# The opening of both feed-forward blocks of an encoder layer, put into one written order with six pairs begun early

## The chip, the cores and the metric

The kernel runs on one core of one Trainium2 chip. The time is the device time of one execution in microseconds (us). TensorE (PE) multiplies matrices, with a weight load (PEld) ahead of each matmul; VectorE (DVE) and ScalarE (ACT) work on elements; SyncE (SP) issues most of the transfers (DMA). Each of these engines takes its instructions in the order of its own queue.

## The reference

One layer of a bidirectional encoder, in float32, for two groups of tokens (512 and 256, together 768) of width 1024:

```python
def swiglu(x, w_up, w_down):
    gate, up = jnp.split(x @ w_up, 2, axis=-1)
    return (jax.nn.silu(gate) * up) @ w_down

x = layer_norm(ALPHA * x + 0.5 * swiglu(x, ffn1_up, ffn1_down), ln1_g, ln1_b)
u = x @ w_in
...                       # RWKV-7 branch h_a, retention branch h_b, gates
mix = (jax.nn.sigmoid(gate_a) * h_a + jax.nn.sigmoid(gate_b) * h_b) @ w_out
x = layer_norm(ALPHA * x + mix, ln2_g, ln2_b)
x = layer_norm(ALPHA * x + 0.5 * swiglu(x, ffn2_up, ffn2_down), ln3_g, ln3_b)
```

The hidden width of a feed-forward block is 2816, which is 22 column blocks of 128. The change concerns the two `swiglu` blocks alone, called block 1 and block 2 below.

## The kernel before

**Precision.** Every operand of a large product is kept as two parts, a rounded one (`ph`, `xh`, `eh`) and the rest (`pl`, `xl`, `el`). `split` (L196) makes them: ACT casts the source to the rounded part (L197), then DVE subtracts it from the source (L198). One product is then three sets of matmuls: rounded weights by both parts of the tokens, and the rest of the weights by the rounded tokens.

**Pairs and products.** `ffn` (L310) works on 22 pairs, one for each block of 128 hidden columns: the gate and the up weights of that block. The inner width (8 slabs of 128) and the tokens (768) are each cut in two, so the tokens are four quarters: B11 and B21 are the first 384 tokens of slabs 0-3 and 4-7, B12 and B22 the last 384 tokens. A pair's 2x2 by 2x2 product is done with seven products instead of eight, from sums of quarters and sums of weight halves. A product takes 4 slabs, so it has 12 matmuls over 384 tokens. They are numbered as in the code: 1 and 2 use plain weights and B11, B21; 5, 7, 6, 3 use weight sums (made by `combine`, L357, on DVE into `sa` tiles) with the token forms T1, T3, T2 and with B22; 4 uses plain weights with the form T4.

**Token forms.** `forms` (L290) makes T1 to T4 once a block: 16 DVE subtractions (4 slabs by 4 forms), and a split of each result, which is 16 casts on ACT and 16 subtractions on DVE, all of 128x384. In block 1 twelve splits of token quarters come on top (L1262); in block 2 the layer norm ahead of it has made them.

**Order.** A planner, which knows the durations only by a model, orders the instructions of each engine by readiness, with older ones first. Where `manual_schedule` is used (L524) PE, ACT and DVE keep the written order among the instructions of that region; how these fall among others of the same engine stays with the planner. Before the change, the loads, the token forms and the products 1 and 2 of the first four pairs (`head` L362, `second` L371, LEAD = 4) stand ahead of the region, so the planner orders them. The region (`body`, L483) runs a list of items, one product each. In its step t it does this: `post` of item t-1 (copies, SiLU and additions from PSUM), loads, weight sums that are needed some items later, the weight split (`prep`) of item t+2, the late part of item t-1, and the matmuls of item t. An early pair has five items left (5, 7, 6, 3, 4), another pair has seven. The weight pieces have four buffers each, raw weights ten. After each chunk of pairs (6, 6, 5, 5) come the items of the down product (`down_items`).

**Around block 2.** Layer norm 2 (L264, in two halves of 384 tokens) ends just as block 2 begins. The weights of block 2 are loaded once the buffers of the stage before are free, and PSUM is handed from one pool to the next.

Of the kernel before, what the change touches and what calls it, by code (L numbers as in the profile page):

```python
# [18 lines left out]
P = 128  # L19
# [36 lines left out]
LEAD = 4  # L56
# [13 lines left out]
class Builder:  # L70
# [219 lines left out]
    def forms(self, z, xs, ext, tmp):  # L290
        nc = self.nc
        m = KT // 2
        sub = lambda o, a, b: nc.vector.tensor_tensor(out=o, in0=a, in1=b, op=ALU.subtract)
        B = [[t[:, c:c + TH] for t in (z[k], z[k + m]) for c in (0, TH)] for k in range(m)]
        ta = [tmp.tile([P, T], F32, tag="hh", name=self.nm("f")) for k in range(m)]
        for k, (b11, b12, b21, b22) in enumerate(B):
            sub(ta[k][:, :TH], b12, b11)
            self.split(ta[k][:, :TH], *(t[:, TH:] for t in xs[k]))
        tb = [tmp.tile([P, T], F32, tag="hl", name=self.nm("f")) for k in range(m)]
        for k, (b11, b12, b21, b22) in enumerate(B):  # L300
            sub(tb[k][:, :TH], b22, b12)
            self.split(tb[k][:, :TH], *(t[:, :TH] for t in ext[k]))
        for k, (b11, b12, b21, b22) in enumerate(B):
            sub(ta[k][:, TH:], b22, ta[k][:, :TH])
            self.split(ta[k][:, TH:], *(t[:, 2 * TH:] for t in ext[k]))
        for k, (b11, b12, b21, b22) in enumerate(B):
            sub(tb[k][:, TH:], b21, ta[k][:, TH:])
            self.split(tb[k][:, TH:], *(t[:, TH:2 * TH] for t in ext[k]))

    def ffn(self, ctx, z, xs, idx, up, down, after, lead, first, then=None):  # L310
# [6 lines left out]
        hs, raws, open_ = {}, {}, {}  # L317
# [25 lines left out]
        def load(j, part):  # L343
            if (j, part) not in raws:
                raws[j, part] = raw(up[j, :, part])
            return raws[j, part]
# [7 lines left out]
        def product(ps, w, x, start):  # L354
            self.mmt(ps, self.terms(pieces(w), X[x]), ((0, TH),), start, True, not start)

        def combine(a, b, op):  # L357
            t = fw.tile([P, m * P], F32, tag="sa", name=self.nm("sa"), bufs=4)
            nc.vector.tensor_tensor(out=t, in0=a, in1=b, op=op)  # L359
            return t  # L360

        def head(j):  # L362
            g = load(j, 0)
            s, uu = (hp.tile([P, T], F32, tag=t, name=self.nm("u")) for t in ("hh", "hl"))
            ps = self.bank()[:, :TH]
            product(ps, g[0], "11", True)
            nc.scalar.copy(uu[:, :TH], ps)  # L367
            open_[j] = s, uu, ps
            return g

        def second(j, g):  # L371
            s, uu, ps = open_[j]
            product(ps, g[1], "21", False)
            nc.scalar.activation(s[:, :TH], ps, AF.Silu)

        def pair_items(j):
            early = j in open_
            st = {}

            def sums(names):  # L380
                def run():
                    (g0, g1), (u0, u1) = load(j, 0), load(j, 1)
                    for n in names:
                        if n == 1:
                            st[1] = combine(u0, u1, ALU.add)
                        elif n == 3:
                            st[3] = combine(g0, u0, ALU.subtract)
                        elif n == 2:
                            st[2] = combine(st[1], g0, ALU.subtract)
                        else:  # L390
                            st[4] = combine(g1, st[2], ALU.subtract)
                return run

            if early:
                st["s"], st["u"] = open_[j][:2]
# [11 lines left out]
            src = {1: lambda: load(j, 0)[0], 2: lambda: load(j, 0)[1], 4: lambda: load(j, 1)[1],  # L407
# [26 lines left out]
            def after_late(n):  # L434
                if n == 4:
                    nc.vector.tensor_tensor(out=hs[j][1], in0=st["s"], in1=hs[j][0].bitcast(F32), op=ALU.subtract)
                    for k in ((j, 0), (j, 1)):
                        raws.pop(k)

            items = []  # L440
            of = {5: 1, 7: 3, 6: 2, 3: 4}
            for n in (5, 7, 6, 3, 4) if early else (1, 5, 7, 6, 2, 3, 4):
# [4 lines left out]
                need = (sums((of[n],)), 3 if early else 6 + (n in (6, 3))) if n in of else None  # L447
                items.append((src[n], mm, *(lambda n=n, f=f: f(n) for f in (post, late, after_late)), need))
            return items, lambda: (load(j, 0), load(j, 1))

        def down_items(ci):
            ch = chunks[ci]
            items, fetch = [], []
            for n in range(KT):
                got = {}
                for i, c in enumerate(range(0, len(ch), m)):
# [22 lines left out]
                    items.append((get, mm, post, none, none, None))  # L479
                    fetch.append(get)  # L480
            return items, fetch

        def body():  # L483
            items, fetch, extra, mixed = [], {}, {}, []
            for ci, ch in enumerate(chunks):
                for q, j in enumerate(ch):
                    its, get = pair_items(j)
# [89 lines left out]
        if then:  # L577
            then()
# [778 lines left out]
```

## Time and profile before

| | |
|---|---|
| median of 3 runs | 1981.83 us (1980.63 to 1992.86) |
| profiled execution: its own time | 1982.73 us |
| its span, first to last instruction | 1981.0 us |
| PE busy | 1886.8 us (95%) |
| DVE busy | 1259.4 us (64%) |
| ACT busy | 807.0 us (41%) |
| mean granted clock of PE | 0.979 |
| block 1: first matmul, start of the 43rd product | 5.80, 107.07 us |
| block 2: first matmul, start of the 43rd product | 1431.88, 1527.43 us |

Busy times are sums over the span. An instruction's duration includes the tail of its pipeline, so an engine that issues without a pause has starts that are closer together than its durations are long. In rows of the timeline, the columns are the start, the duration, the engine, the line, the operation, the tiles written and read, the shapes and the count; a bracket at the end tells how long the engine stood idle before it, and what released it. Rows of stretches (windows) give, after the length, the busy time and the number of instructions of PE, PEld, DVE, ACT and POOL, then the granted clock, the share of the DMA engines and GB/s.

### The profile page before, as it was taken

How to read it: one execution, taken by the hardware profiler on the slowest of the kernel's cores; microseconds unless marked ns; L12 is line 12 of the kernel's file. 1: busy time of each engine (PE TensorE's matmuls, PEld its weight loads, DVE VectorE, ACT ScalarE, POOL GpSimd, SP SyncE). 2: the span in 40 equal slices, each digit the busy share in tenths (PEclk: the TensorE clock that was granted, in tenths of full speed). 3: DMA queues.
4: the chain of work that ended last, by engine and by line, in shares of the span. 5: the costliest groups of instructions: out<-in, count | busy, mean ns of one | idle time of the engine just before them, and what ended most of it. 6: DMA issues, size and time to landing. Idle time of an engine off the chain costs nothing.

```text
span 1981.0 us, 33145 instructions
## 1 busy us (share of the span) xinstructions
PE 1886.8 (95%) x13098; PEld 1685.0 (85%) x13098; DVE 1259.4 (64%) x2208; ACT 807.0 (41%) x1521; POOL 190.3 (10%) x290
## 2 busy tenths in 40 slices
PE   7999999999989999999899989999899999999997
PEld 7999999998778778887688867789789899899985
DVE  8855746656745686768445555386797477375655
ACT  6422423323454353545255555332554234132325
POOL 0000000000000365345610000000000000000000
PEclk9999999999989999999999989999999999999998
DMA  5222222121332433333555442654222221222221
GB/s 197 81 69 75 64 75 71 49 85 45 123 103 69 156 115 127 116 128 121 155 164 139 123 121 74 210 163 138 80 77 73 81 69 56 79 63 69 67 70 66
DMA packets 140444, 198.40 MB, mean 100 GB/s; under 512 B 55552, under 2 KB 73600, under 8 KB 140288
## 3 DMA queue, kind: packets, MB, share of 16 engines
q1 hardware_dynamic: 122752, 174.25, 27.8%
q0 software_dynamic: 3424, 14.94, 2.2%
q10 hardware_dynamic: 14112, 7.08, 1.3%
q8 instruction: 104, 1.70, 0.4%
q14 instruction: 52, 0.43, 0.1%
HBM read 154.54 MB, written 41.68 MB: 99 GB/s over the span
## 4 chain that ended last, share of the span: by engine, by line
PE 82%; DVE 9%; ACT 4%; DMA 3%; issue 2%; SPq 0%; ACTq 0%; POOL 0%; DVEq 0%; POOLq 0%
PE mm L208 39%; PE pc L208 30%; PE pc L253 2%; PE mm L630 2%; PE pc L107 2%; PE pc L1046 1%; DMA t<-gd 1%; PE w L982 1%; PE pc L1094 1%; PE pc L687 1%; DVE z L281 1%; PE w L993 1%; DVE u L410 1%; PE w L987 1%; PE pc L1055 1%
## 5 line engine op out<-in xcount | busy, mean ns | idle before, releaser
L208 PE MATMUL pc<-xh,ph 128*128 128x384 f32 x704 | 241.9, 344 | 20.8 <-ACT u L367 6.7
L208 PE MATMUL pc<-xl,ph 128*128 128x384 f32 x704 | 237.8, 338 | 0.1
L197 ACT CAST ph<-wr 128x512 fp32r<-128x512 f32 (+1 forms) x232 | 131.1, 568 | 220.2 <-PE mm L208 140.3
L208 PE MATMUL mm<-xh,wh 128*128 128x512 f32 (+1 forms) x640 | 177.2, 356 | 15.0 <-DVE t L707 5.1
L410 DVE TENSOR_TENSOR u<-u,pc 128x384 f32<-128x384 f32 x220 | 121.6, 553 | 89.1 <-PE pc L208 85.4
L208 PE MATMUL pc<-el,ph 128*128 128x384 f32 x528 | 176.4, 334 | 0.0
L208 PE MATMUL pc<-eh,ph 128*128 128x384 f32 x528 | 176.4, 334 | 0.0
L208 PE MATMUL mm<-xl,wh 128*128 128x512 f32 (+1 forms) x640 | 169.9, 346 | 0.0
L208 PEld LDWEIGHTS pc<-xh,ph 128*128 128x128 f32 x704 | 133.7, 190 | 30.4 <-ACT u L367 8.0
L198 DVE TENSOR_TENSOR pl<-wr,ph 128x512 fp32r<-128x512 f32 (+1 forms) x232 | 141.6, 623 | 20.6 <-ACT ph L197 20.6
L208 PE MATMUL pc<-xh,pl 128*128 128x384 f32 x704 | 151.0, 336 | 0.0
L198 DVE TENSOR_TENSOR pl<-sa,ph 128x512 fp32r<-128x512 f32 x176 | 121.2, 689 | 45.6 <-ACT ph L197 45.4
L208 PE MATMUL mm<-hl,ph 128*128 128x512 f32 (+1 forms) x544 | 138.9, 336 | 0.0
L208 PE MATMUL mm<-hh,ph 128*128 128x512 f32 (+1 forms) x544 | 138.8, 336 | 0.0
L208 PEld LDWEIGHTS pc<-xl,ph 128*128 128x128 f32 x704 | 133.8, 190 | 0.8 <-DVE xl L198 0.7
L169 DVE TENSOR_TENSOR wl<-wr,wh 128x1024 fp32r<-128x1024 f32 (+1 forms) x68 | 74.8, 1100 | 92.7 <-PE mm L208 47.2
L208 PEld LDWEIGHTS mm<-xh,wh 128*128 128x128 f32 x640 | 101.7, 192 | 36.9 <-issue 14.9
L197 ACT CAST ph<-sa 128x512 fp32r<-128x512 f32 x176 | 105.4, 617 | 52.9 <-DVE sa L359 24.9
L208 PEld LDWEIGHTS pc<-xh,pl 128*128 128x128 f32 x704 | 125.7, 189 | 0.0
L208 PE MATMUL mm<-xh,wl 128*128 128x512 f32 (+1 forms) x640 | 124.2, 343 | 0.0
L168 ACT CAST wh<-wr 128x1024 fp32r<-128x1024 f32 (+1 forms) x68 | 62.7, 922 | 139.0 <-PE mm L208 112.7
L208 PEld LDWEIGHTS mm<-xl,wh 128*128 128x128 f32 x640 | 100.6, 192 | 16.8 <-issue 2.5
(311 smaller groups left out, 3926.3 us busy)
## 6 DMA issues: line engine op xcount, KB each, us to landing
wr<-in_f1u SPq DMA_DIRECT2D x96, 256.0 KB, 3.1
wr<-in_f2u SPq DMA_DIRECT2D x96, 256.0 KB, 3.0
wr<-in_w_in SPq DMA_DIRECT2D x30, 512.0 KB, 3.5
wr<-in_f1d SPq DMA_DIRECT2D x37, 256.0 KB, 2.7
wr<-in_f2d SPq DMA_DIRECT2D x37, 256.0 KB, 2.7
wr<-in_w_in SPq DMA_DIRECT2D x32, 256.0 KB, 3.4
dd<-ar SPq DMA_DIRECT2D x8, 768.0 KB, 3.3
dd<-kb SPq DMA_DIRECT2D x8, 768.0 KB, 4.4
```

What stands on the lines that cost most here:

```text
L107: self.nc.tensor.matmul(ps, w, x[:, a:b], start=True, stop=True)
L168: nc.scalar.copy(hi, raw)
L169: nc.vector.tensor_tensor(out=lo, in0=raw, in1=hi.bitcast(F32), op=ALU.subtract)
L197: self.nc.scalar.copy(hi, src)
L198: self.nc.vector.tensor_tensor(out=lo, in0=src, in1=hi.bitcast(F32), op=ALU.subtract)
L208: self.latest = self.nc.tensor.matmul(o, w, x[:, a:b], start=start and i == 0, stop=stop and i == len(terms) - 1, skip_group_check=more).ins
L253: self.summed = nc.tensor.matmul(st["ps"], self.ones, src, start=k == 0, stop=k == KT - 1).ins
L281: nc.vector.scalar_tensor_tensor(out=zk, in0=zk, scalar=-0.5, in1=rs, op0=ALU.mult, op1=ALU.mult)
L410: add = lambda o, a, b: nc.vector.tensor_tensor(out=o, in0=a, in1=b, op=ALU.add)
L630: nc.tensor.matmul(dst, x[:, ts], w[:, :, k % 4], start=(k == 0 and q == 0), stop=(k == KT - 1 and q == 2))
L687: nc.tensor.matmul(op, v[:, a // P + j], x[:, j, :n], start=(j == 0 and q == 0), stop=(j == nj - 1 and q == 2))
L982: nc.tensor.matmul(pb[64 * h:64 * h + 64, C * j:C * j + C], sc[:, c % 4, h, 1], vu[:, c % 4, h], start=True, stop=True)
```

## The change

The opening moves into the region. `forms` no longer issues anything: it returns a list of single steps. A step is either the start of one form (for T1 to T4 the DVE operation and the cast on ACT, for plain quarters the cast alone) or the DVE subtraction that ends it; each subtraction stands behind the start of the next form. A new function, `advance`, issues steps in the region's step t, behind the weight split of item t+2: up to three DVE operations a step from t = 4 in block 1 (`own` is True: it also splits its own quarters) and from t = 6 in block 2, and more where an item's form would otherwise be missing.

LEAD becomes 6. The list begins with twelve items, products 1 and 2 of pairs 0 to 5 in the order OPEN, then takes the early pairs two at a time: 5, 5, 7, 7, 6, 6, 3, 4, 3, 4. Full pairs have the order 1, 5, 7, 6, 2, 3, 4 with nothing of another pair mixed in. T2 is made as T3 + B11 instead of B22 - T1, and T4 as B21 - T2, as before. Sums of early pairs overwrite their `sa` tile; product 6 of an early pair goes to another PSUM bank. Raw weights are loaded by halves, and the gate weights of six early pairs are loaded twice (of four before). In block 1 the weight and token loads have a new order, and the constants are loaded in step 100.

```diff
-LEAD = 4
+LEAD = 6
+OPEN = [(1, 0), (1, 1), (1, 2), (1, 3), (2, 0), (2, 1), (1, 4), (1, 5), (2, 2), (2, 3), (2, 4), (2, 5)]
+FORMS = {True: 4, False: 6}
...
-    def forms(self, z, xs, ext, tmp):
+    def forms(self, z, xs, ext, tmp, own):
...
+        rows = []
+        if own:
+            rows += [("11", None, B[k][0], part(xs, k, 0)) for k in range(m)]
+            rows += [("21", None, B[k][2], part(xs, k + m, 0)) for k in range(m)]
+        ta, tb = half("hh"), half("hl")
+        rows += [("T1", tt(ta[k], B[k][1], B[k][0], ALU.subtract), ta[k], part(xs, k, TH)) for k in range(m)]
+        rows += [("T3", tt(tb[k], B[k][3], B[k][1], ALU.subtract), tb[k], part(ext, k, 0)) for k in range(m)]
+        rows += [("T2", tt(tb[k], tb[k], B[k][0], ALU.add), tb[k], part(ext, k, 2 * TH)) for k in range(m)]
+        if own:
+            rows += [("22", None, B[k][3], part(xs, k + m, TH)) for k in range(m)]
+        rows += [("T4", tt(tb[k], B[k][2], tb[k], ALU.subtract), tb[k], part(ext, k, TH)) for k in range(m)]
+        steps, late = [], None
+
+        def low(src, hi, lo):
+            return lambda: nc.vector.tensor_tensor(out=lo, in0=src, in1=hi.bitcast(F32), op=ALU.subtract)
+
+        for name, make, src, (hi, lo) in rows:
+            def begin(make=make, src=src, hi=hi):
+                if make:
+                    make()
+                nc.scalar.copy(hi, src)
+            if late and name == "21" != late[0]:
+                steps.append(late)
+                late = None
+            steps.append((name, begin, bool(make), False))
+            if late:
+                steps.append(late)
+            late = name, low(src, hi, lo), True, True
+        return steps + [late]
...
-                    st[key] = self.bank()[:, :TH]
+                    st[key] = self.mmps()[:, :TH] if early and n == 6 else self.bank()[:, :TH]
...
-            for n in (5, 7, 6, 3, 4) if early else (1, 5, 7, 6, 2, 3, 4):
+            for n in (1, 5, 7, 6, 2, 3, 4):
...
+            early = [pair_items(j) for j in range(LEAD)]
+            items += [early[j][0][n] for n, j in OPEN]
+            for j in range(0, LEAD, 2):
+                pair = early[j:j + 2]
+                fetch.setdefault(len(items), []).extend(p[1] for p in pair)
+                items += [p[0][n] for n in (5, 7, 6) for p in pair] + [p[0][n] for p in pair for n in (3, 4)]
...
+            steps = self.forms(z, xs, ext, hp, own)
+
+            def advance(t):
+                x = items[t][7] if 0 <= t < len(items) else None
+                names = [n for n, *_ in steps]
+                must = len(names) - names[::-1].index(x) if x in names else 0
+                begin = FORMS[own]
+                n = 0
+                while steps and (must > 0 or n < (3 if t >= begin else 0) or steps[0][0] == "11"
+                                 or steps[0][0] == "21" and t >= 0 and n < 2):
+                    name, f, vector, _ = steps.pop(0)
+                    f()
+                    n += vector
+                    must -= 1
...
                     prep(t + 2)
+                    advance(t)
                     if t > 0:
                         items[t - 1][3]()
...
-        first(load, ext, hp)
-        for j in range(lead):
-            second(j, head(j))
-            raws.pop((j, 0))
+        if start:
+            start(load)
...
             for a in (0, TH):
-                load(a // TH, 0)
-                for k in range(KT):
-                    zk = z[k][:, a:a + TH]
-                    nc.sync.dma_start(zk, I["xT"][:, k, a:a + TH])
-                    if a == 0 or k >= KT // 2:
-                        self.split(zk, *(t[:, a:a + TH] for t in xs[k]))
-            self.forms(z, xs, ext, tmp)
+                for h in range(2):
+                    load(0, 0, h)
+                    for k in range(KT // 2 * h, KT // 2 * (h + 1)):
+                        nc.sync.dma_start(z[k][:, a:a + TH], I["xT"][:, k, a:a + TH])
+                    if a == 0:
+                        for j in range(1, 4 - 2 * h):
+                            load(j, 0, h)
```

More of the change, by code (lines that the diff above doesn't have):

```diff
@@ L303, in forms @@
[L303 to L310, printed above, removed]
+        part = lambda ts, k, c: tuple(t[:, c:c + TH] for t in ts[k])
@@ L311, in ffn @@
+        return steps + [late]
+    def ffn(self, ctx, z, xs, idx, up, down, after, start, own, then=None):
         nc = self.nc
@@ L341, in wide, with load @@
             return tuple(t.rearrange("p (a b) -> p a b", b=P) for t in (h, l))
[L343 to L346, printed above, removed]
+        def load(j, part, h):
+            if (j, part, h) not in raws:
+                raws[j, part, h], = raw(up[j, :, part, h * m:h * m + m])
+            return raws[j, part, h]
         def pieces(src):
@@ L352, in pieces @@
             return tuple(t.rearrange("p (a b) -> p a b", b=P) for t in (h, l))
[L354 to L359, printed above, removed]
-            return t
[L362 to L374, printed above, removed]
+        def combine(a, b, op, out=None):
+            t = fw.tile([P, m * P], F32, tag="sa", name=self.nm("sa"), bufs=4) if out is None else out
+            self.mark = nc.vector.tensor_tensor(out=t, in0=a, in1=b, op=op).ins
+            return t
         def pair_items(j):
-            early = j in open_
+            early = j < LEAD
@@ L378, in pair_items, with sum_of @@
             st = {}
-            def sums(names):
+            def sum_of(n):
                 def run():
[L382 to L391, printed above, removed]
-                return run
@@ L394, in pair_items @@
-            if early:
-                st["s"], st["u"] = open_[j][:2]
+                    g0, g1, u0, u1 = [load(j, p, h) for p in range(2) for h in range(2)]
+                    if n == 1:
+                        st[1] = combine(u0, u1, ALU.add)
+                    elif n == 3:
+                        st[3] = combine(g0, u0, ALU.subtract)
+                    elif n == 2:
+                        st[2] = combine(st[1], g0, ALU.subtract, st[1] if early else None)
+                    else:
+                        st[4] = combine(g1, st[2], ALU.subtract, st[2] if early else None)
@@ L446, in mm @@
                     self.mmt(ps, self.terms(w, X[xof[n]]), ((0, TH),), n not in (2, 3, 4), True, n in (2, 3, 4))
-                need = (sums((of[n],)), 3 if early else 6 + (n in (6, 3))) if n in of else None
-                items.append((src[n], mm, *(lambda n=n, f=f: f(n) for f in (post, late, after_late)), need))
-            return items, lambda: (load(j, 0), load(j, 1))
+                    if early and n < 3:
+                        raws.pop((j, 0, n - 1))
+                need = (sum_of(of[n]), 3 if early else 6 + (n in (6, 3))) if n in of else None
+                get = (lambda n=n: load(j, 0, n - 1)) if early and n < 3 else None
+                items[n] = src[n], mm, *(lambda n=n, f=f: f(n) for f in (post, late, after_late)), need, get, xof[n]
+            return items, lambda: [load(j, p, h) for p in range(2) for h in range(2)]
         def down_items(ci):
             ch = chunks[ci]
-            items, fetch = [], []
+            items = []
             for n in range(KT):
@@ L530, in body @@
                     ahead(t)
+                    if then and t == 100:
+                        with self.tc.issue_after(self.mark):
+                            then()
                     for f in extra.get(t, ()):
@@ L1246, in build @@
                      lambda seg, mean, lp: self.layer_norm(lp, z, 3, None, seg, mean, O["y"]),
-                     LEAD, lambda load, ext, tmp: self.forms(z, self.xs, ext, tmp))
+                     None, False)
     def first(self, ctx):
```

57 lines of the change are left out of this document (20 added, 37 removed).

## The prediction

> **What bounds the kernel now.** I read the page first, then stretches of both openings, then who PE waited for in them, then the timeline engine by engine.
>
> ```profile
> span 1981.0 us, 33145 instructions
> PE 1886.8 (95%) x13098; PEld 1685.0 (85%) x13098; DVE 1259.4 (64%) x2208; ACT 807.0 (41%) x1521; POOL 190.3 (10%) x290
> ...
> 5.80:16.20 10.40, 6.88 (x24) 5.54 (x24) 9.17 (x19) 7.81 (x16) 0.00 (x0) 1.00 1.01 347
> 16.20:35.94 19.74, 17.79 (x84) 17.47 (x85) 19.74 (x45) 14.37 (x31) 0.00 (x0) 0.83 0.55 188
> 35.94:107.07 71.13, 69.79 (x398) 68.42 (x397) 59.92 (x99) 27.16 (x49) 0.00 (x0) 1.00 0.27 85
> 1431.88:1444.40 12.52, 9.40 (x51) 8.76 (x52) 12.48 (x26) 11.40 (x24) 0.00 (x0) 1.00 0.14 44
> 1444.40:1456.31 11.91, 10.59 (x59) 9.95 (x58) 11.91 (x26) 9.42 (x21) 0.00 (x0) 1.00 0.14 45
> 1456.31:1527.43 71.12, 69.78 (x397) 68.41 (x397) 61.40 (x100) 27.66 (x50) 0.00 (x0) 1.00 0.27 86
> ...
> 37.33 0.85 PE L208 MATMUL pc<-eh,pl 128*128 128x384 f32 x4
> 39.41 0.85 PE L208 MATMUL pc<-eh,pl 128*128 128x384 f32 x4
> ```
>
> PE is the bound of the kernel as a whole, and the openings are where it is not fed. The last two rows are the same place of two products that follow each other: one product costs 39.41 - 37.33 = 2.08 us. In block 1 the first two stretches hold 24 + 84 = 108 matmuls, which are 9 products of 12, in 30.14 us instead of 18.7. The next one holds 33 more in 71.13 us, where 33 x 2.08 = 68.6. So product 43 begins at 107.07, and the 42 products of six pairs cost 107.07 - 5.80 = 101.3 us against 87.4 at full rate: 13.9 lost. In block 2 they cost 1527.43 - 1431.88 = 95.6: 8.2 lost. All that better feeding can give is about 22 us, 1.1% of the time. The same rows name the engine behind it: from 16.20 to 35.94 and from 1431.88 to 1456.31 DVE is busy without a pause.
>
> ```profile
> PE pc L208 <- ACT xh L197: 5.8, 1, 5.8
> PE pc L208 <- ACT u L367: 4.3, 2, 3.8
> PE pc L208 <- DVE u L410: 1.3, 2, 1.2
> PE pc L208 <- ACT ph L197: 1.1, 1, 1.1
> ...
> PE pc L208 <- issue: 2.5, 1, 2.5
> PE pc L208 <- ACT u L367: 2.4, 2, 1.6
> PE pc L208 <- ACT ph L197: 1.5, 1, 1.5
> ...
> 17.59 0.69 PE L208 MATMUL pc<-xh,ph 128*128 128x384 f32 x1 [3.76 <-ACT u L367]
> ...
> 18.71 0.52 PE L208 MATMUL pc<-xl,ph 128*128 128x384 f32 x1
> 19.03 0.52 PE L208 MATMUL pc<-xh,ph 128*128 128x384 f32 x1
> ...
> 1443.19 0.44 PE L208 MATMUL pc<-xh,ph 128*128 128x384 f32 x1 [1.59 <-ACT u L367]
> ...
> 1443.65 0.34 PE L208 MATMUL pc<-xh,ph 128*128 128x384 f32 x1
> 1443.82 0.35 PE L208 MATMUL pc<-xl,ph 128*128 128x384 f32 x1
> ...
> 1431.16 0.62 DVE L243 SCALAR_TENSOR_TENSOR ln<-pc,eps,ln 128x384 f32<-128x384 f32 x1
> ...
> 1431.88 0.41 PE L208 MATMUL pc<-xh,ph 128*128 128x384 f32 x1 [2.52 <-issue]
> ```
>
> The first four rows are PE's waits in block 1, the next three those in block 2 (time in all, times, longest). The copy of product 1 (L367) sits on ACT behind casts of the forms, and product 2 adds to the bank it reads. The gap of 3.76 costs twice: behind it matmuls are 0.32 apart (18.71 to 19.03), behind the gap of 1.59 they are 0.17 apart. The 2.5 put down to "issue" in block 2 ends 0.1 us after L243, the last reader of layer norm 2's bank; PSUM changes hands there, the change doesn't touch it, so block 2 still begins at 1431.88.
>
> **What the change removes.** With twelve products in a row that need neither forms nor sums, a copy has at least three products before product 2 of its pair, so the waits on L367 go, 4.3 and 2.4 us, and with them the slow clock behind 17.59. The two extra reloads of gate weights a block are covered: DMA engines are busy 0.14 to 0.27 of these stretches.
>
> **What it adds: a written order between DVE and ACT.** The count of DVE and ACT operations stays the same, 32 DVE operations for the forms (block 1 has 12 more for its own quarters). What changes is that they stand in fixed places. In a step, DVE does the weight subtraction, then three form operations. ACT does the copy or SiLU of the last product, the weight cast, then the casts of the forms. The next weight cast on ACT thus stands behind the last form's cast, which waits for DVE, and DVE's next weight subtraction waits for that weight cast. Before, the planner was free to issue casts whose sources were long ready. The lengths:
>
> ```profile
> 1432.40 3.84 DVE L281 SCALAR_TENSOR_TENSOR z<-z,ln 128x384 f32<-128x384 f32 x8
> 52.61 0.68 DVE L359 TENSOR_TENSOR sa<-wr,wr 128x512 f32<-128x512 f32 x1
> 53.21 0.69 DVE L198 TENSOR_TENSOR pl<-wr,ph 128x512 fp32r<-128x512 f32 x1
> 61.59 1.73 DVE L410 TENSOR_TENSOR u<-u,pc 128x384 f32<-128x384 f32 x3
> ...
> 12.04 0.55 DVE L293 TENSOR_TENSOR f<-z 128x384 f32<-128x384 f32 x1
> 12.62 0.52 ACT L197 CAST xh<-f 128x384 fp32r<-128x384 f32 x1 [0.54 <-DVE f L293]
> ...
> 1443.78 3.43 ACT L197 CAST eh<-f 128x384 fp32r<-128x384 f32 x8
> ...
> 1455.82 0.49 ACT L374 ACTIVATE u<-pc 128x384 f32<-128x384 f32 x1 [2.46 <-PE pc L208]
> 1456.21 0.61 ACT L197 CAST ph<-sa 128x512 fp32r<-128x512 f32 x1
> ...
> 56.22 1.13 ACT L197 CAST ph<-sa 128x512 fp32r<-128x512 f32 x2
> 56.85 0.69 DVE L198 TENSOR_TENSOR pl<-sa,ph 128x512 fp32r<-128x512 f32 x1 [0.50 <-ACT ph L197]
> ...
> 1449.10 1.28 ACT L374 ACT_TABLE_LOAD   x1
> ```
>
> Start to start, a DVE operation of 384 costs (3.84 - 0.55) / 7 = 0.47, one of 512 costs 53.21 - 52.61 = 0.60. A form's result reaches ACT 0.03 after its 0.55 are over (12.59 to 12.62). A cast on ACT lets the next begin after (3.43 - 0.51) / 7 = 0.42, a SiLU or copy after 0.39 (1455.82 to 1456.21), and a weight subtraction starts 0.63 after its cast started (56.22 to 56.85). That last row is the very wait in small: DVE idle, released by a cast that stood behind other work on ACT.
>
> If the step's three form operations are start, end, start, the next weight subtraction comes 0.60 + 0.47 + 0.47 + 0.55 + 0.03 + 0.42 + 0.39 + 0.63 = 3.56 us later; if end, start, end, it is 0.60 + 0.47 + 0.55 + 0.03 + 0.42 + 0.39 + 0.63 = 3.09. The two alternate. Weight sums (0.60) fit in the idle part. PE uses a step in 2.08, so PE falls back by about 1.25 us a step once the lead of two products is used up. Products 5 and 7 have no copy, so steps behind them cost 0.39 less: 3.17 and 2.70.
>
> The Trainium skill, "VectorE: DVE Perf Modes", section Terms, has each DVE operation wait until the pipeline of the one before is empty. By that, starts would be 0.55 apart and about 1.8 us a block would come on top; the eight operations at 1432.40 are 0.47 apart, so the trace disagrees and the sum goes by 0.47.
>
> **Block 2.** From 1431.88, six products are 12.5 us; ACT has layer norm 2's end there beside casts and copies (11.40 of 12.52 busy before, with 1.5 lost to ph), of which I keep half: step 6 begins at 1445.1. Its weight subtraction waits for the copy, and starts 1.2 later (0.16 tail of the product, 0.39, 0.63). Steps 6 to 11 add 3 x 3.09 + 3 x 3.56 = 19.95, steps 12 to 15 add 2.70 + 3.17 + 2.70 + 3.17 = 11.74. Step 16 ends the forms (0.60 + 2 x 0.47), then come the three additions of product 6 (1.73), which must be through before product 3 may add to the bank that they read. So item 18 begins 1.2 + 19.95 + 11.74 + 1.54 + 1.73 = 36.2 after 1445.1, at 1481.3, where twelve products at full rate would be 25.0. From there DVE keeps up (ten items of two pairs need 10 x 0.60 for weights, 8 x 0.60 for sums, 2 x 1.73 and 4 x 0.47 for additions, and four operations of 768, as two of 384 each 0.94: 19.9 of 20.8). With 24 x 2.08 = 49.9, and 0.9 for the small gaps that 71.13 - 68.6 holds, product 43 begins at 1532.1: **4.7 later** than 1527.43.
>
> **Block 1.** The order of loads changes, so I need its rate:
>
> ```profile
> 0.00:10.00 10.00, 4.12 (x12) 3.49 (x12) 5.13 (x15) 5.98 (x10) 0.21 (x4) 1.00 0.76 258
> 10.00:20.00 10.00, 5.18 (x22) 4.48 (x21) 9.41 (x20) 8.58 (x19) 0.00 (x0) 0.85 1.02 353
> ```
>
> The first product is held by the arrival of the quarters, before (12 matmuls in the first 10 us) as after; three more at 2.08 bring PE to item 4 at about 16.3, where before it had done two products and stood waiting until 17.59, with the slow clock to come. Step 4 needs the weights of pair 4, which are loaded behind 16 token quarters of 0.19 MB and six weight halves of 0.25: 5 MB, at 2.58 MB in the first 10 us and 0.35 a us then, about 18.3 (an estimate from these two rows). Its weight subtraction starts at 18.9. Steps 4 to 11 add 4 x 3.56 + 4 x 3.09 = 26.6, and 1.28 for the table load of the first SiLU in step 5. Step 12 has three ends with nothing to wait for, 0.60 + 0.60 + 3 x 0.47 = 2.6; then 2.70, 3.17, 2.70. Step 16 and the additions are 0.60 + 0.47 + 1.73 = 2.8. Item 18 begins at 18.9 + 27.9 + 11.2 + 2.8 = 60.8, and product 43 at 60.8 + 49.9 + 0.9 = 111.6: **4.5 later**. What PE gains up to item 4 it gives back in items 8 to 18, where each step costs 3.1 to 3.6 instead of 2.08.
>
> **Sum.** 4.7 + 4.5 = 9.2 us slower. The profiled execution took 1982.73, 1.7 above its span and 0.9 above the median; 1981.8 + 9.2 = **1991**. Behind product 43 both orders are the same; the constants, moved to step 100, are hidden there (DVE 59.92 of 71.13) and cost nothing if that holds.
>
> **Rivals.** (B) DVE is never held by ACT and only its own length counts: a step costs 0.60 + 3 x 0.47 = 2.0, or 2.6 with a weight sum. For it: DVE without a pause from 16.20 to 35.94 at 0.44 an operation. Against it: the 0.50 at 56.85, in written order. Block 1: 18.9 + 5 x 2.08 + 7 x 2.6 + 2.8 + 50.8 = 101.1, 6.0 sooner; block 2: 1445.1 + 1.2 + 3 x 2.08 + 7 x 2.6 + 3.3 + 50.8 = 1524.8, 2.6 sooner. In all **1973**. It decides if ACT has its casts done when DVE turns to a step.
>
> (C) Even this is absorbed and only the start's losses remain: some 10 and 5 us sooner, **1967**. Against it: DVE without slack in both openings.
>
> (D) Pauses of 1.3 us in every 3.3 halve PE's clock, as behind 17.59. A product then lasts 12 x 0.32 = 3.84 instead of the step's 3.3, ten items cost 5 us more in each block: **2001**. Against it: the gap of 1.59 in block 2 left the rate as it was. The Trainium skill, "TensorE: Matmul & The Clock Gate", section "A second HAM failure mode: psum-queue depth-cycling", tells of a kernel whose frequent short idle times between groups of matmuls made the clock fall back and return; no run here shows that yet.
>
> (E) The planner sets the instructions around block 2 otherwise, and the parts cancel: **1982**.
>
> **Numbers.** A 0.50, B 0.27, C 0.08, D 0.10, E 0.05. The range 1969 to 1999 holds A with errors of 8 either way, B and E, and leaves out C and most of D. Within 1% (1962 to 2001.6, about what a measurement can tell from no change) lies nearly everything: faster by more needs more than C gives, 0.03; slower by more takes the worse half of D, 0.06.
>
> **What would show it.** Right: PE unbroken from 5 to 16 and no slow matmuls at 18; then products about 3.3 us apart for ten items, PE waiting for `pl` or `ph`, and DVE idle more than 1 us a step, released by ACT ph; item 18 near 61, and 36 us behind item 6 in block 2; product 43 at about 111.6, and 100.2 behind the first in block 2. Wrong: DVE without idle time in these steps (B), matmuls 0.32 apart in items 8 to 18 (D), or product 43 of block 1 before 107.

## The result, and the profile after

The changed kernel takes **2002.94 us**, the median of 6 runs (1999.83 to 2006.55), against 1982.82 for the kernel before in 6 runs beside them. The ratio is 1.0094, with a 95% interval of 1.0069 to 1.0118: 14 to 23 us slower. Forecast were 1991 us and a range of 1969 to 1999. The sign was right and the size about half of what came.

The profiled execution took 1999.83 us. Its page begins with the span and the busy time of each engine, in us, with the share of the span and the instructions:

```profile
span 1998.0 us, 33175 instructions
PE 1891.1 (95%) x13098; PEld 1686.9 (84%) x13098; DVE 1261.1 (63%) x2208; ACT 809.4 (41%) x1521; POOL 190.4 (10%) x290
```

The work is the same: 13098 matmuls, 2208 DVE operations, busy times within 5 us. The span is 17.0 us longer, so PE waits more. The next view cuts the span at the starts of products. Items of the list are counted from 0 and products from 1, so product 43, the 43rd, is item 42; item 18 is the one that the code numbers 3 in the first pair. The cuts are the first product of block 1, its items 4, 10 and 18, product 43, the first product of block 2, item 10 of it, its item 18, its product 43, the end. The columns are the stretch in us, its length, then the busy time of PE, PEld, DVE, ACT and POOL with instructions, the granted clock of PE, the DMA share and GB/s.

```profile
5.00:16.84 11.84, 11.75 (x48) 10.30 (x49) 7.02 (x13) 7.43 (x15) 0.00 (x0) 1.00 0.99 323
16.84:34.30 17.46, 14.49 (x73) 13.86 (x72) 8.75 (x18) 9.16 (x17) 0.00 (x0) 0.90 0.69 229
34.30:61.85 27.55, 18.67 (x97) 16.46 (x97) 23.77 (x45) 12.98 (x27) 0.00 (x0) 1.00 0.21 67
61.85:114.11 52.26, 52.08 (x289) 51.52 (x290) 47.52 (x78) 19.04 (x33) 0.00 (x0) 0.97 0.30 91
114.11:1442.81 1328.70, 1265.53 (x9642) 1100.57 (x9641) 816.42 (x1462) 556.96 (x1047) 190.14 (x286) 0.98 0.35 110
1442.81:1464.88 22.07, 21.20 (x121) 20.89 (x121) 14.44 (x27) 17.23 (x33) 0.00 (x0) 1.00 0.26 84
1464.88:1493.09 28.21, 18.83 (x97) 16.29 (x97) 23.92 (x46) 12.36 (x25) 0.00 (x0) 0.99 0.20 66
1493.09:1545.10 52.01, 51.83 (x289) 51.27 (x289) 47.49 (x78) 19.02 (x33) 0.00 (x0) 0.97 0.29 91
1545.10:1998.00 452.90, 436.70 (x2451) 405.73 (x2450) 271.31 (x449) 152.92 (x290) 0.00 (x0) 0.98 0.22 69
```

Product 43 begins at 114.11 instead of 107.07 (+7.0), and in block 2 at 1545.10 - 1442.81 = 102.29 after the first product instead of 95.55 (+6.7). Between the openings stand 1328.70 instead of 1324.81 (+3.9), and the tail is 0.7 shorter. That makes 17.0, the difference of the spans. The third and seventh rows hold most of the loss against the full rate: 97 matmuls need 97 x 0.173 = 16.8 us at full rate and take 27.55 and 28.21.

The waits of PE, in block 1 first, then in block 2 (waited for: us in all, times, longest):

```profile
PE pc L210 <- ACT xh L320: 5.0, 1, 5.0
PE pc L210 <- ACT ph L199: 4.5, 6, 1.2
PE pc L210 <- DVE u L409: 3.3, 1, 3.3
PE pc L210 <- DVE xl L314: 3.0, 1, 3.0
...
PE pc L210 <- ACT ph L199: 5.5, 8, 1.2
PE pc L210 <- DVE u L409: 4.2, 1, 4.2
PE pc L210 <- issue: 2.5, 1, 2.5
```

The waits for the copy (u, L367 before) are gone, as forecast. In their place stand many short waits for `ph`, the weight cast on ACT, and a single long one for `u`, the three additions of product 6, which must be through before item 18 may add to its bank.

The wait of 3.0 for `xl` in block 1 is at item 4, and these rows of ACT, DVE and PE show what it waited for:

```profile
18.85 0.62 ACT L199 CAST ph<-wr 128x512 fp32r<-128x512 f32 x1 [1.33 <-DMA wr<-in_f1u]
...
19.50 0.69 DVE L200 TENSOR_TENSOR pl<-wr,ph 128x512 fp32r<-128x512 f32 x1 [2.32 <-ACT ph L199]
...
20.58 0.55 DVE L314 TENSOR_TENSOR xl<-z,xh 128x384 fp32r<-128x384 f32 x1
...
21.18 0.50 PE L210 MATMUL pc<-xl,ph 128*128 128x384 f32 x1 [2.97 <-DVE xl L314]
```

The weights at 18.85 are those of pair 4, which item 6 needs. In the written order the last subtraction of a plain quarter (20.58) stands behind their subtraction (19.50) and the start of a form, so item 4 waits for a load that it doesn't use.

The timeline shows one step of block 1, from one weight subtraction to the next (start, length, engine, line; in brackets how long the engine had stood idle and what released it):

```profile
37.86 0.69 DVE L200 TENSOR_TENSOR pl<-wr,ph 128x512 fp32r<-128x512 f32 x1 [0.87 <-ACT ph L199]
37.88 0.45 PE L210 MATMUL pc<-xh,ph 128*128 128x384 f32 x1 [1.22 <-ACT ph L199]
...
38.47 0.55 DVE L314 TENSOR_TENSOR el<-f,eh 128x384 fp32r<-128x384 f32 x1
...
38.93 0.55 DVE L295 TENSOR_TENSOR f<-f,z 128x384 f32<-128x384 f32 x1
...
39.40 0.55 DVE L314 TENSOR_TENSOR el<-f,eh 128x384 fp32r<-128x384 f32 x1
39.52 0.51 ACT L320 CAST eh<-f 128x384 fp32r<-128x384 f32 x1 [1.70 <-DVE f L295]
39.87 0.68 DVE L376 TENSOR_TENSOR sa<-wr,wr 128x512 f32<-128x512 f32 x1
39.94 0.48 ACT L420 ACTIVATE u<-pc 128x384 f32<-128x384 f32 x1
40.32 0.61 ACT L199 CAST ph<-sa 128x512 fp32r<-128x512 f32 x1
40.96 0.69 DVE L200 TENSOR_TENSOR pl<-sa,ph 128x512 fp32r<-128x512 f32 x1 [0.41 <-ACT ph L199]
40.98 0.44 PE L210 MATMUL pc<-xh,ph 128*128 128x384 f32 x1 [0.72 <-ACT ph L199]
```

This is the chain that was forecast: end, start, end on DVE, then the form's cast (39.52, released by DVE 0.04 after 39.48), the SiLU (39.94), the weight cast (40.32), and with its end both PE and the next subtraction. ACT had stood idle for 1.70 ahead of it. The step is 40.96 - 37.86 = 3.10 long; products here begin at 34.30, 37.88, 40.98, 44.55 and 47.66, so 3.58, 3.10, 3.57 and 3.11 apart (items 10 to 14).

### The profile page after: what moved, and what is told of

It reads as the page before. It is cut to its first block, busy times and chain, and to the rows that moved or that the text cites. A ratio compares the mean times of both kernels' runs of the same rounds, so it can differ in the third digit from the quotient of the medians.

```text
span 1998.0 us, 33175 instructions
## 1 busy us (share of the span) xinstructions
PE 1891.1 (95%) x13098; PEld 1686.9 (84%) x13098; DVE 1261.1 (63%) x2208; ACT 809.4 (41%) x1521; POOL 190.4 (10%) x290
## 4 chain that ended last, share of the span: by engine, by line
PE 79%; DVE 9%; DMA 4%; ACT 4%; issue 2%; SPq 0%; ACTq 0%; DVEq 0%; POOLq 0%
PE mm L210 39%; PE pc L210 28%; PE pc L255 2%; PE mm L644 2%; PE pc L109 2%; PE pc L1060 1%; DMA t<-gd 1%; PE w L996 1%; ACT ph L199 1%; DVE u L409 1%; PE pc L1108 1%; PE w L1007 1%; PE pc L701 1%; DVE f L295 1%; DVE z L283 1%
## 5 line engine op out<-in xcount | busy, mean ns | idle before, releaser
L210 PE MATMUL pc<-eh,ph 128*128 128x384 f32 x480 | 161.1, 336 | 2.7 <-ACT ph L199 2.7
L409 DVE TENSOR_TENSOR u<-u,pc 128x384 f32<-128x384 f32 x208 | 114.9, 552 | 76.9 <-PE pc L210 73.8
L210 PE MATMUL pc<-el,ph 128*128 128x384 f32 x480 | 160.5, 334 | 0.0
L210 PEld LDWEIGHTS mm<-xl,wh 128*128 128x128 f32 x640 | 100.9, 193 | 16.8 <-issue 2.5
```

Of the source, the lines that this page charges most:

```text
L210: self.latest = self.nc.tensor.matmul(o, w, x[:, a:b], start=start and i == 0, stop=stop and i == len(terms) - 1, skip_group_check=more).ins
L409: add = lambda o, a, b: nc.vector.tensor_tensor(out=o, in0=a, in1=b, op=ALU.add)
```

## Experiments

Two theories stood at the start. **A**: in each step the next weight cast on ACT waits behind a form's cast, which waits for DVE, and this round trip sets the pace. **B**: the length of DVE's own work sets it. Two more questions came out of the trace: what the long wait ahead of item 18 costs, and whether the stretch between the blocks belongs to the change.

### The round trip taken out of each step (d1)

A form's cast goes onto a list (`pend`) and is issued in the next step, by `flush`, behind that step's weight cast; the subtraction that ends the form comes after it. The operations are the same. In block 1 the edit moves one thing more: the last subtraction of a plain quarter, which the changed kernel issues behind the weight subtraction of step 4, is issued ahead of it.

```diff
         for name, make, src, (hi, lo) in rows:
+            if name not in ("11", "21"):
+                rest.append((name, make, lambda hi=hi, src=src: nc.scalar.copy(hi, src), low(src, hi, lo)))
+                continue
...
+            def flush():
+                for name, cast, low in pend:
+                    cast()
+                    lows.append((name, low))
+                pend.clear()
...
             def advance(t):
...
+                flush()
...
+                    if lows:
+                        lows.pop(0)[1]()
+                        n += 1
+                    elif rest and (n < quota or x in [r[0] for r in rest]):
+                        name, make, cast, low = rest.pop(0)
+                        if make:
+                            make()
+                            n += 1
+                        pend.append((name, cast, low))
```

> The changed kernel, with one thing undone: the cast of a form is no longer issued in the step that makes the form, but in the next step, behind that step's weight cast. Same operations, same quota of three DVE operations a step. Theory A (each step pays one trip from DVE to ACT and back, because the weight cast stands behind the last form's cast): steps fall from 3.1 to 3.6 us to what DVE needs, 2.0 to 2.6; in block 2 item 18 begins 29 us behind item 6 instead of 36.5, in block 1 near 54 instead of 61.9, with no slow matmuls behind it; total 8 to 9 us less for each block, about 1985. Theory B (it is the load of DVE or ACT, not the order): item 18 stays within 2 us of where it was, and the time within 4 us of the changed kernel.

The timeline of d1 at the same place:

```profile
33.93 0.68 DVE L200 TENSOR_TENSOR pl<-sa,ph 128x512 fp32r<-128x512 f32 x1
...
34.15 0.61 ACT L199 CAST ph<-sa 128x512 fp32r<-128x512 f32 x1
...
34.53 1.49 DVE L295 TENSOR_TENSOR f<-f,z 128x384 f32<-128x384 f32 x3
...
35.11 1.45 ACT L318 CAST eh<-f 128x384 fp32r<-128x384 f32 x3 [0.35 <-DVE f L295]
...
36.54 0.68 DVE L200 TENSOR_TENSOR pl<-sa,ph 128x512 fp32r<-128x512 f32 x1
...
20.00:48.68 28.68, 28.55 (x164) 27.92 (x162) 28.19 (x55) 19.60 (x42) 0.00 (x0) 1.00 0.49 157
```

The weight cast (34.15) now stands ahead of the form casts (35.11), and the next weight subtraction (36.54) finds it done. From 20.00 to 48.68, the last row, PE is busy for 28.55 of 28.68 us. Item 18 begins at 51.52 instead of 61.85, and in block 2 28.7 after item 6 instead of 36.5. In block 1 it begins 28.4 after item 6 (23.16) instead of 36.0 (25.83). So the same operations in another order make this stretch 7.7 us shorter in block 1 and 7.8 in block 2; in block 1 item 6 itself comes 2.7 earlier, without the wait at item 4. That is A's round trip; DVE is busy for 28.19 of the same 28.68 us, and its weight subtractions are 36.54 - 33.93 = 2.61 apart, so what is left is B's length of 2.6. Product 43 begins at 103.77 and, in block 2, 94.81 after the first, in both blocks earlier than in the kernel before. The time is 1983.28 (10 runs, 1980.61 to 1990.32), a ratio of 1.0004 to the kernel before, interval 0.9991 to 1.0017: by the ratios 18 us less than the changed kernel, and no difference from before. What was missed: the wait ahead of item 18 stayed, at 2.84 and 3.25, and slow matmuls behind it.

### The forms left to the planner (d3)

```diff
             ahead(0)
+            while steps:
+                steps.pop(0)[1]()
             with self.tc.manual_schedule(engines={E.Activation, E.DVE, E.PE}):
```

> One part of the change alone: twelve products first and the early pairs two at a time, but all the steps of the token forms issued ahead of the region, so that the planner orders them as it did before. Theory A: no step of 3.1 to 3.6 us, item 18 of block 2 at most 31 us behind item 6; waits of PE for weight casts or copies at the start, as before the change (some 3 us a block); total 1975 to 1990. Theory B (the twelve products first and the pairs by two are what costs): as slow as the changed kernel, 1998 or more.

Everything else of the change stands, but the forms aren't part of the written order. The waits of PE in block 1:

```profile
PE pc L210 <- ACT ph L199: 5.2, 3, 4.6
```

In block 1 there is no wait for `u`, and none for `ph` in the steps. The loss sits in one place, 4.6 ahead of item 3 at 18.99, where the weight cast stands behind casts of the forms. In block 2 it sits in two, 2.5 for `ph` at item 3 and 1.7 for a copy (`u`) at item 6, so item 6 comes later there, 18.6 after the first product instead of 13.75. Item 18 begins at 52.88, in block 2 25.1 after item 6; product 43 begins at 103.54 and 94.43. The time is 1984.14 (10 runs, 1974.08 to 1988.66), a ratio of 0.9999, interval 0.9983 to 1.0015. So neither the six early pairs, the order of the list nor the loads made the openings long: the places of the form steps did.

### Twice as many steps at a time (d2)

```diff
-                while steps and (must > 0 or n < (3 if t >= begin else 0) or steps[0][0] == "11"
+                while steps and (must > 0 or n < (6 if t >= begin else 0) or steps[0][0] == "11"
```

> The changed kernel with up to six DVE operations of the forms in a step instead of three. Theory A (the trip to ACT and back is paid once a step, whatever the number of operations): five products of the opening are 4.8 to 5.0 us apart (0.60 + 5 x 0.47 + 0.55 + 1.47), and those after them 2.1; item 18 of block 2 begins 35 to 36.5 us behind item 6, with no wait of over 2 us ahead of it. Rival (it is paid by operation): each step of six takes 6.7 us, twice the 3.33 of a step of three.

Once the lead is used up, products of block 1 begin at 39.09, 43.61 and 48.12: steps of 4.5. In block 2 they begin at 1467.65, 1472.62, 1477.60 and 1482.57: steps of 4.97. Rows of the timeline, two weight subtractions one step apart in block 1, and two in block 2:

```profile
43.59 0.69 DVE L200 TENSOR_TENSOR pl<-wr,ph 128x512 fp32r<-128x512 f32 x1 [0.41 <-ACT ph L199]
...
48.09 0.69 DVE L200 TENSOR_TENSOR pl<-sa,ph 128x512 fp32r<-128x512 f32 x1 [0.40 <-ACT ph L199]
...
1472.60 0.69 DVE L200 TENSOR_TENSOR pl<-wr,ph 128x512 fp32r<-128x512 f32 x1 [0.87 <-ACT ph L199]
...
1477.58 0.69 DVE L200 TENSOR_TENSOR pl<-sa,ph 128x512 fp32r<-128x512 f32 x1 [0.87 <-ACT ph L199]
```

In block 1 the last but one of a step's six form operations is a start, and the prediction's own sum gives 0.60 + 4 x 0.47 + 0.55 + 0.03 + 0.42 + 0.39 + 0.63 = 4.50; measured are 48.09 - 43.59 = 4.50. In block 2 the last of the six is a start, so one more operation stands ahead of the last cast: 4.97 by the sum, and 1477.58 - 1472.60 = 4.98 measured. The expectation of 4.8 to 5.0 had this second case alone. Twice the operations cost 1.41 us more a step (4.50 against 3.09, 4.97 against 3.56), which is three times 0.47, and not twice as much: each step pays for one round trip, whatever is in it, and the rival's 6.7 us a step did not come. The forms are through sooner, and there is no wait ahead of item 18, but PE lost the time in front instead: in block 1 23.06 us from item 6 to item 12 (25.06 to 48.12), where the changed kernel has 15.15 (25.83 to 40.98), with a clock of 0.85 on average behind waits of 2.15 and 2.14. Item 18 begins at 62.27, and in block 2 36.84 after item 6, where the changed kernel has 61.85 and 36.53; expected for block 2 were 35 to 36.5. The one execution took 1999.53.

### A product more ahead of item 18 (d4)

Item 17's product is issued twice, which fills the wait ahead of item 18 with work and moves nothing else.

```diff
-                        items[t][1](ready.pop(t))
+                        w = ready.pop(t)
+                        for _ in range(2 if t == 17 else 1):
+                            items[t][1](w)
```

> The changed kernel with the twelve matmuls of item 17 issued twice (the same sums again), so that PE works for 2.1 us of the 3.3 and 4.2 us for which it stands still ahead of item 18. Theory G (the long standstill lets the clock fall): matmuls of item 18 are 0.17 apart, item 19 begins 2.1 us behind item 18 instead of 3.5, and the span is 2.8 us less. Rival (item 18 is slow for a reason of its own, as its bank): still 3.5 us, and the span the same.

The timeline of PE at item 18 in the changed kernel, and then in d4:

```profile
61.85 0.41 PE L210 MATMUL pc<-xh,ph 128*128 128x384 f32 x1 [3.29 <-DVE u L409]
...
62.81 0.53 PE L210 MATMUL pc<-xh,ph 128*128 128x384 f32 x1
63.13 0.53 PE L210 MATMUL pc<-xl,ph 128*128 128x384 f32 x1
```

```profile
61.81 0.41 PE L210 MATMUL pc<-xh,ph 128*128 128x384 f32 x1 [1.20 <-DVE u L409]
...
62.41 0.33 PE L210 MATMUL pc<-xl,ph 128*128 128x384 f32 x1
62.58 0.33 PE L210 MATMUL pc<-xh,ph 128*128 128x384 f32 x1
```

Item 18 begins at the same time, 61.81, since the additions release it. Behind the wait of 3.29 matmuls are 0.32 apart, behind that of 1.20 0.17. Item 19 follows 3.52 later in the changed kernel and 2.16 later in d4. In block 2 the wait becomes 2.13 instead of 4.20, and item 19 follows 2.15 later instead of 3.50. Product 43 begins at 112.48 instead of 114.11, and in block 2 at 100.96 instead of 102.29: with a product **more** to do, it is there 1.6 and 1.3 sooner. The span is 1992.1, 5.9 less instead of the 2.8 expected: 3.0 less in the openings, 4.1 less between the blocks (1324.60 instead of 1328.70), which the edit doesn't touch, and 1.2 more at the end. This is one execution. A second trace of the changed kernel (r2, below), whose matmuls stayed fast behind item 18's wait, has product 43 at 112.69. So the length of that wait costs twice, as the prediction had seen it in the kernel before.

### The steps spread out (d6)

The edit of d1, with the forms begun a step earlier in block 1 and two earlier in block 2, and only two operations a step from item 9, so that the additions of product 6 don't find a full queue.

```diff
-                quota = 3 if t >= FORMS[own] else 0
+                quota = (3 if t < 9 else 2) if t >= (3 if own else 4) else 0
```

> The kernel with the form's cast behind the next step's weight cast, and the forms begun earlier and spread: from step 3 in block 1 and step 4 in block 2 (4 and 6 there), three DVE operations a step up to step 8, two from step 9 (three throughout there). Theory A: DVE has caught up when the additions of product 6 fall due, so the wait of 2.8 to 3.3 us ahead of item 18 goes, and the slow matmuls behind it too: about 4.2 us less for each block than that kernel; product 43 near 99.5 in block 1 and 90.6 behind the first of block 2; the openings 12 us under the kernel before, and the time, with 3 to 5 us more between the blocks as in the other changed kernels, 1971 to 1979. Rival (the wait ahead of item 18 is for something else than DVE's backlog): it stays, and the time is 1980 to 1985.

The stretches of block 1's opening, between the blocks, and of block 2's opening:

```profile
4.99:101.67 96.68, 93.40 (x505) 90.49 (x505) 86.08 (x151) 48.88 (x91) 0.00 (x0) 1.00 0.45 149
101.67:1427.19 1325.52, 1264.29 (x9641) 1100.34 (x9641) 815.87 (x1462) 556.74 (x1047) 189.42 (x286) 0.98 0.35 110
1427.19:1518.34 91.15, 89.98 (x504) 88.81 (x505) 84.75 (x149) 48.48 (x90) 0.00 (x0) 0.98 0.29 92
```

The wait ahead of item 18 is 1.7 and 1.0 and the clock holds behind it. Product 43 begins at 101.67, and 91.15 after the first in block 2, where 87.4 would be full rate and 99.5 and 90.6 were expected; in block 1 a wait of 0.8 for a form's subtraction (`el`, L314) is left at item 19. The time is 1978.80 (12 runs, 1972.91 to 1991.62), a ratio of 0.9973 to the kernel before, interval 0.9947 to 0.9999. It is clearly faster than the changed kernel; that it is faster than the one before is likely, but that interval all but touches 1.

### Is it lateness? (c1)

The kernel before, with one product of three full pairs of block 1 issued twice: 36 matmuls more, behind the opening.

```diff
-                    self.mmt(ps, self.terms(w, X[xof[n]]), ((0, TH),), n not in (2, 3, 4), True, n in (2, 3, 4))
+                    for _ in range(2 if then and n == 5 and j in (7, 8, 9) else 1):
+                        self.mmt(ps, self.terms(w, X[xof[n]]), ((0, TH),), n not in (2, 3, 4), True, n in (2, 3, 4))
```

> The kernel before, with three products of block 1 done twice (product 5 of pairs 7, 8, 9: 36 matmuls more, nothing else). It shows what the stages between the blocks do when they only begin later. If they depend on nothing but their start: 6.2 us more, about 1989, and 1324.8 us from product 43 of block 1 to block 2 less the 0 that this moves, plus 6.2. If their order or their transfers change with the start, as the 3 to 4 us between the blocks in the changed kernel suggest: 2 us or more beyond the 6.2, 1991 or more.

36 x 0.173 = 6.2 us of work were added and 8.7 came out (ratio 1.0044, interval 1.0025 to 1.0063, so 5.0 to 12.5). The interval holds 6.2, while the median, 1990.90, lies at the edge of the other reading (1991 or more). Its one trace has 1335.30 us from product 43 to block 2, 9.1 more than before's four traces below have on average. That a mere delay is paid back with more behind it isn't shown; up to 6 us of it isn't excluded either.

### Both kernels again (r1 to r6)

Both kernels, unchanged, three more executions each, for the spread of a single trace. r1 and r2 ran on the chip of the experiments above, r3 to r6 on another.

> The kernel before, unchanged, for a second trace. If the stage between the blocks (1324.8 us from product 43 of block 1 to the first product of block 2) varies by itself from execution to execution, it differs by 2 us or more here; if it is fixed for a program, by less than 1.

> The changed kernel, unchanged, for a second trace. Openings: within 0.5 us of the first trace (product 43 at 114.1; 102.3 behind the first product of block 2). Between the blocks: 1328.7 us in the first trace; 2 us or more off if that stage varies by itself, less than 1 if not.

> The kernel before, unchanged, a third trace, for the stretch between the blocks (from product 43 of block 1 to the first product of block 2; 1324.8 and 1324.1 us so far). If that stretch only varies by chance, before and changed kernel overlap over their four traces each; if the changed kernel's other order in the scan stage costs time, the kernel before stays under 1326 here.

> The changed kernel, unchanged, a third trace, for the same stretch (1328.7 and 1331.7 us so far). By chance: anything from 1324 to 1336. By its order: above 1327 again. The openings as before, with the slow matmuls of item 18 there or not.

> The kernel before, a fourth trace, as the third: under 1326 us between the blocks again if the order decides; spread over 1324 to 1336 if chance does.

> The changed kernel, a fourth trace, as the third: above 1327 us between the blocks if the order decides; spread over 1324 to 1336 if chance does.

With the two first executions, there are four traces of each:

| us | before | changed |
|---|---|---|
| time of the execution | 1982.73, 1981.32, 1989.33, 1981.17 | 1999.83, 2002.54, 2000.02, 2003.13 |
| product 43, block 1 | 107.07, 106.51, 106.67, 106.50 | 114.11, 112.69, 113.44, 114.41 |
| between the openings | 1324.8, 1324.1, 1332.0, 1323.7 | 1328.7, 1331.7, 1326.0, 1329.9 |
| product 43 after the first, block 2 | 95.6, 96.2, 96.3, 95.5 | 102.3, 103.7, 103.5, 102.9 |

The openings repeat within 2 us (0.5 was expected of r2, whose openings are off by 1.4) and differ by 7.0 and 7.2 on average, 14.2 together, with no overlap. The stretch between them is 2.9 longer on average, but it overlaps: the longest of before (r3) is longer than all of the changed kernel, and the shortest of the changed kernel (r4) is under the 1327 that its own order would have meant. r3 and r5, 8.3 apart, are one kernel on one chip. That row of r3, and the shortest of the changed kernel, r4's:

```profile
106.67:1438.63 1331.96, 1268.41 (x9642) 1103.02 (x9641) 814.10 (x1449) 555.14 (x1044) 188.84 (x286) 0.97 0.35 109
```

```profile
113.44:1439.39 1325.95, 1260.75 (x9641) 1096.22 (x9641) 816.56 (x1462) 556.96 (x1047) 190.26 (x286) 0.98 0.35 110
```

The same matmuls take 1268.41 in one and 1260.75 in the other, at a clock of 0.97 and 0.98: much of this spread is the clock. One pair of traces could not have told it from the change, and four of each don't show how much of the 2.9 belongs to it.

**What stays open.** The timed ratios leave more than the openings explain. Against the means of before's four traces, the openings of d1, d3 and d6 are 4.0, 4.6 and 9.8 shorter, those of the changed kernel 14.2 longer. By the ratios the times differ by +0.8, -0.2, -5.4 and +18.6 us. In each of the four, 4 to 5 us come on top. Each interval is 2.6 to 5.2 wide to either side and d1 and d3 share their runs of before, so this is likely rather than shown. Two parts are seen. In the first 20 us behind product 43 PE is busy throughout before and stands 0.46 in the changed kernel, 0.45 in block 2. Block 1's row of the changed kernel:

```profile
114.11:134.11 20.00, 19.54 (x112) 18.57 (x112) 15.30 (x24) 9.80 (x18) 0.00 (x0) 1.00 0.23 69
```

That is 0.9 of it. And an execution is longer than its span: by 1.77 on average in the kernel before (21 runs beside d1 and d3), by 1.95 in the changed kernel, 2.24 in d1, 2.28 in d3 and 2.35 in d6, so 0.2 to 0.6 lie outside the spans. In the scan stage between the blocks, VectorE's operations have the same order in d3 as in the kernel before, and another one in the changed kernel; d3 shows the excess as well, so another order there doesn't explain it. One candidate is open: the mean granted clock is 0.9796 over those 21 runs of before and 0.9767, 0.9769 and 0.9755 in d1, d3 and the changed kernel. If PE had work throughout the time at the lower clock, 0.003 x 1981 would be some 6 us (an estimate from these means); but in d6 it is 0.9783 against 0.9787 beside it, with the same excess. Where the other 3 to 4 us sit was not found.

## Why the prediction was wrong, and where it was right

**The mechanism was right.** A had steps of 3.56 and 3.09; products are 3.58, 3.10, 3.57 and 3.11 apart. d1 takes the round trip out of the order and the openings become shorter than before; d2 follows the same sum to 0.01 in both blocks, 4.50 and 4.97. B is refuted as a forecast: DVE stands idle for 3.8 of 27.55 us in the steps, released by ACT. The sign "DVE idle more than 1 us a step" was too large: it is 0.41 and 0.87, since the weight sums (L376) stand in that time.

**The start was nearly right.** PE is unbroken from 5.00 to 16.84 as forecast. The weights of pair 4 are there at 18.85 instead of 18.3, and their subtraction starts at 19.50 instead of 18.9 (the 5 MB of the prediction leave out pair 4's own two halves; by the two rows 5 MB alone are there at 16.9, and 5.5 at 18.3); item 18 begins at 61.85 instead of 60.8. In block 2 item 6 comes 13.75 after the first (forecast 13.2) and item 18 36.5 after it (36.2). Up to item 18 the two sums are off by 1.0 and 0.9 us. "No slow matmuls" did not hold: item 4 waited 2.97 in the middle, behind pair 4's weight subtraction, a wait that the prediction didn't have, and matmuls behind it were 0.32 apart. By the prediction's sum it cost little by itself, since the steps of DVE and ACT, which begin with that subtraction, set item 18: 42.35 us lie between the two, where the sum has 41.9.

**The first failed step is the term behind item 18.** The prediction let the rest run at full rate from the moment that item 18 begins: "With 24 x 2.08 = 49.9, and 0.9". It had not worked out how long PE waits ahead of it. That follows from its own terms: item 17's product is through some 2 us after it starts, while DVE still owes step 16 and 1.73 us of additions. The wait was 3.29 and 4.20, and its own row of 3.76 in the kernel before shows what stands behind such a wait. The term measured 52.26 and 52.01 instead of 50.8, and d4 shows it as the clock: with the shorter wait it is 50.67 in both blocks. That is 1.5 and 1.2 us. With the errors ahead of item 18, the two openings came to +13.8 in this pair of traces instead of +9.2.

**Rival D had the right cause at the wrong place.** It let the pauses of 1.3 us in every step halve the clock. They did not: granted is 1.00 from 34.30 to 61.85, with pauses of 0.72 and 1.22 in turn. So the fallback that the Trainium skill describes in "TensorE: Matmul & The Clock Gate", section "A second HAM failure mode: psum-queue depth-cycling", did not come with pauses of this size.

**The second failed step is "Behind product 43 both orders are the same".** In this pair of traces +3.2 us come from there (3.9 - 0.7). By four traces each, the stretch between the blocks is 2.9 longer on average, within a spread of 8.3 that the kernel before has by itself; 0.9 is seen as waits where the early pairs hand over to the full ones (ahead of item 43), and the 4 to 5 us that the ratios leave are open as to their cause. The waits at the hand-over could have been forecast, the order there being part of the change.

**The third lies in the range.** It was built on 8 us to either side of A, while the executions of one kernel lay 12 us apart in the table that the prediction had (1980.63 to 1992.86), and up to 22 in the runs beside d6 (1978.53 to 2000.75). Of the 11.9 us that the forecast was short, 4.6 are the openings, 3.2 lie behind product 43, 3.1 are the median's distance from the profiled execution, which was the shortest of six, and 0.9 are the prediction's step from the execution to the median of before. Of the difference between the kernels, 18.6 us by the ratio against 9.2 forecast, four traces each give 14.2 to the openings, 5.0 more than forecast, and 4.4 are the open rest.

## What to carry to other kernels

When work of two in-order engines that feed each other is written into fixed steps, each step pays for a whole round trip between them, however little is in it; issue what waits for the other engine one step later, behind the work that the bottleneck waits for, and the round trip is gone (d1: 7.7 us a block from item 6 to item 18, with the same operations). Then work out how long the bottleneck stands ahead of each join, since a wait of about 3 us can cost another 1.4 in slow matmuls. And compare several traces of each kernel before giving a few microseconds of a long stretch to a cause.

## What the runs showed of the hardware

The clock falls neither always nor at one length of wait. Behind item 18's wait, matmuls became 0.32 apart in three of four traces of block 1 (3.29, 3.28, 3.27) and stayed 0.17 apart in the fourth. In block 2 (4.20 to 4.23) they became slow in all four. The one that stayed fast had waited 3.27 too (r2). In the kernel before, one trace was not slow behind 3.23 (r3). In d2, matmuls that had been 0.17 apart became slow behind waits of 2.14 and 2.15, while behind one of 2.13 in d4 they stayed fast.

Where it falls, it often does so only after PE has begun again. In d1, where PE had been busy for 28.55 of the 28.68 us ahead, it waited 2.84; the first matmuls behind that are 0.17 apart and those from 52.59 on 0.32:

```profile
51.52 0.41 PE L210 MATMUL pc<-xh,ph 128*128 128x384 f32 x1 [2.84 <-DVE u L413]
...
52.91 0.52 PE L210 MATMUL pc<-xh,ph 128*128 128x384 f32 x1
53.23 0.52 PE L210 MATMUL pc<-xl,ph 128*128 128x384 f32 x1
```

The Trainium skill, "TensorE: Matmul & The Clock Gate", section "What's actually happening", has the half rate after at least one idle window of about 3.4 us, in windows that run on freely. The free-running window would fit the same wait of 3.27 to 3.29 with both outcomes. That a whole window must be idle does not fit these traces: d1's wait of 2.84, with work right ahead of it, is shorter than that window, as are the 2.14 and 2.15 of d2.

What stood out beside it is the spread of one program: the same kernel before took 1323.7 to 1332.0 us for the same 9642 matmuls between the blocks.
